# Arithmetic of GpSimd moved to VectorE before the feed-forward and in its last superblock of a hybrid decoder layer

## The chip, the cores and the metric

The kernel runs on one core of a Trainium2 chip. The metric is device time in microseconds (us) of one execution. Engines: TensorE (PE; its weight loads are listed as PEld), VectorE (DVE), ScalarE (ACT), GpSimd (POOL), SyncE (SP, which here only issues DMAs).

## The reference, cut to what matters

One decoder layer for a prompt of 2048 positions and 8 samples of 4 positions, all float32, width 1024:

```python
h = rms_norm(x, norm_mix); z = h @ w_in                       # u | xin | B | C, 512 each
y_ssm = s5_ssm(u, ...)                                        # 32 groups, 64 complex states, scan over time
y_ssm = gelu(y_ssm); y_ssm = y_ssm * sigmoid(y_ssm @ w_glu + b_glu)
y_conv = B * causal_dwconv(C * xin, conv_w)                   # width 3
x = x + concat(rms_norm(y_ssm), rms_norm(y_conv)) @ w_out
x = x + cross_attention(rms_norm(x, norm_xattn), k, v)        # 4 heads, 256 memory tokens
h = rms_norm(x, norm_ffn)
x = x + (gelu(causal_dwconv(h @ w_up)) * (h @ w_gate)) @ w_down   # 2816 wide
y = rms_norm(x, norm_final)
```

## The kernel before, in words

Positions are split into 5 pieces of up to 416 columns (`NPC`, `NP`). Every product is made at float32 accuracy from three matmuls (`mm3`, lines 365 to 367): each operand is split into a rounded `hi` and a remainder `lo`, and hi*hi, hi*lo and lo*hi are summed. So each weight tile and each activation tile costs a cast and a subtraction ahead of its matmuls:

- `Weights` (class of line 70 on): `issue` starts DMAs into 3 buffers `wraw` through SP, `split` has ACT cast a 128x1024 tile to `whi` (L94) and two subtractions make `wlo` in halves of 512 columns (L98). Both halves go to POOL, except where `share` is true: then the second goes to DVE. `pump` is called once per `block()`, `get` forces a split.
- `Acts`: `issue` loads a 128x416 tile `araw` through SP (L176), `pump` and `put` make `xh` on ACT and `xl`. Even tiles with a gain: `xh` by L161, `xl` by one DVE instruction (L162). Odd tiles: ACT first scales `araw` in place (L191), casts it (L158), and POOL subtracts (L159).

There is no scheduler: each engine runs its instructions in the order in which the code emits them, and waits at the first whose inputs are not ready. Side work is written as generators (`bg`, `slow`, `slow2`), and hooks between the matmuls advance them by a step. So the place of every side instruction among the matmuls is fixed when the program is built. All loads and most stores go through SP's queue, in that order too: a store whose data is late holds up the loads behind it.

Stages, by the time of the profile:

1. 0 to about 200 us, input projection of `u`. `p1_stream` transposes x on PE, splits it, and sums squares. `tables` computes the transition tables of the state space: per quarter `c` a complex product `pk` on DVE (`cmul`, L552 to L558), transposes on PE, and products `ogt`, `og` on POOL (`gtt`, L577). `rstd` makes row scales through diagonal tiles `dgh` on DVE and `dgl` on POOL (L426). `u_out` scales u on POOL (L786, L792) and stores it.
2. About 200 to 575 us, the other three projections, with a convolution per channel tile (`conv_in`, `conv_mid`, `conv_out`; the last multiplication of y is on POOL, L1272, and then y is stored). Beside it run `state_inputs` (`turn`, every third on POOL, L945 to L948; `scan_blocks` on DVE, L955), `toeplitz` (a copy `to` on POOL, L1039) and `state_outputs` (`back`, three DVE instructions and one on POOL, L1063 to L1067; `enter`, two additions `scat` on DVE and two on POOL, L1079, which PE waits for).
3. 575 to 675 us, keys and values of the memory (`memory`), the GLU (`p3_pre`) and its first piece; to about 900 us output projection (`residual_linear`), with `p3_pre` of the next piece beside it, partly on POOL.
4. To about 1500 us attention, then its output projection beside the samples' attention (`sample_attention`, `split` with a part on POOL, L1764).
5. From about 1500 us the feed-forward, 22 tiles of 128 channels for each of three superblocks of pieces (two pieces, two pieces, one). `f_down` multiplies into two PSUM banks `d` in turn; DVE adds each into `xac` (L2037), and PE cannot refill a bank before that. The third superblock, with one piece, uses each weight tile half as long as the others.

Of the kernel before, what the change touches and what calls it, by code (L numbers as in the profile page):

```python
# [71 lines left out]
class Weights:  # L72


    def __init__(self, nc, pool):
        self.nc, self.pool = nc, pool
        self.specs, self.raw, self.slots = [], {}, {}
        self.nraw = self.nsplit = self.nrel = self.now = 0
        self.age, self.share = 2, True
# [10 lines left out]
    def split(self):  # L90
# [31 lines left out]
class Acts:  # L122
# [5 lines left out]
    def __init__(self, nc, pool):  # L128
# [5 lines left out]
        self.age = 2  # L134
# [45 lines left out]
    def pump(self, n=1, force=False):  # L180
        self.now += 1
        self.issue()
        for _ in range(n):
# [5 lines left out]
            eng = self.nc.gpsimd if i % 2 else None  # L189
# [19 lines left out]
def tile_hymba_step(ctx: ExitStack, tc: tile.TileContext, I: dict, O: list):  # L209
# [201 lines left out]
    def rstd(pl, rs, acc, p, n, lag=3):  # L411
# [148 lines left out]
    def tables():  # L560
# [15 lines left out]
        def gtt(out, a, b, op):  # L576
            G.tensor_tensor(out=out, in0=a, in1=b, op=op)  # L577
# [106 lines left out]
        for m in (1, 2, 4):  # L684
# [3 lines left out]
                 pa[:, 0, m:m + 1, :].to_broadcast(sh), pa[:, 1, m:m + 1, :].to_broadcast(sh), sh, f"cm{m}", G)  # L688
            yield PAUSE
        G.tensor_copy(out=a4, in_=pa[:, :, 4, :])  # L690
        G.tensor_copy(out=mg, in_=mag)
        G.tensor_scalar(out=qc[:, 0], in0=cm, scalar1=1.0, scalar2=None, op0=ALU.add)
        G.tensor_copy(out=qc[:, 1], in_=sn)
# [85 lines left out]
    def u_out(p, us):  # L779
        yield PAUSE  # L780
        w, c0 = CW[p], CPP * p
        for j in range(4):
            u = us[j]
            cols = slice(j * 128, (j + 1) * 128)
            if p < 4:
                G.tensor_tensor(out=u, in0=u, in1=rs_p[p], op=ALU.mult)  # L786
                store(out=u_d[cols, :, c0:c0 + w], in_=u[:, 0:8 * w].rearrange("p (s c) -> p s c", s=8))
            else:
                e = ends[j % 2]
                for o, a, n in ((e[:, :, 0:w], 0, 8), (e[:, 0:NT, w:w + 8], 384, NT), (e[:, NT:8, w + 8:w + 16], 384, NT)):  # L790
                    z = slice(a, a + n * (w if a == 0 else 8))
                    G.tensor_tensor(out=o, in0=u[:, z].rearrange("p (s c) -> p s c", s=n),  # L792
# [18 lines left out]
    W.age, W.share = 6, False  # L811
# [145 lines left out]
    def state_inputs():  # L957
# [16 lines left out]
        def recur(upto, n):  # L974
# [5 lines left out]
            for _ in range(n):  # L980
# [3 lines left out]
                if turned < upto:  # L984
                    turn(turned, G if turned % 3 == 1 else V)
# [1162 lines left out]
```

## Time and profile before

| what | before |
|---|---|
| median of 3 runs | 3034.99 us (3028.71 to 3035.61) |
| the profiled execution | 3038.51 us, its span 3036.7 us |
| PE busy | 2891.9 us, 95% |
| DVE, POOL, ACT busy | 1474.0, 1152.2, 1112.6 us |
| PE busy, 0 to 683 us and after | about 86%, 98% |
| mean granted clock of PE | 0.977 |

The time is read from two things: where PE, the busiest engine, stands idle or at the lower of its two clock levels, and what ends those waits. "Released by" below means the semaphore event that came last before an instruction started.

### The profile page before, as it was taken

To read this page: it belongs to the slowest core of one execution; us is meant where nothing else is said; L and a number is where in the kernel's file an instruction comes from. 1 tells how busy PE (TensorE), PEld (TensorE's weight loads), DVE (VectorE), ACT (ScalarE), POOL (GpSimd) and SP (SyncE) were. 2 spreads that over 40 slices of the span, in tenths; PEclk is the share of its full clock that TensorE was granted. 3 is DMA by queue.
4 is the path that set the end of the run, shared out by engine and by line. 5 is a ranking of instruction groups with operands and counts; after the bars stand their busy time and mean duration, and the time that the engine had idled before them with its cause. 6 is when DMAs were issued, how large, how long until landed. Compare 5 with 4: busy or idle time off the path is not lost.

```text
span 3036.7 us, 41679 instructions
## 1 busy us (share of the span) xinstructions
PE 2891.9 (95%) x15536; PEld 2792.3 (92%) x15536; DVE 1474.0 (49%) x2704; ACT 1112.6 (37%) x2168; POOL 1152.2 (38%) x1264
## 2 busy tenths in 40 slices
PE   7877979989999999999999999999999999999998
PEld 7777969879999999989999999998999999999998
DVE  5758786354354343454543333435433433354544
ACT  5344333454544444342522222234222222243332
POOL 3664475353341004252523232233232233245653
PEclk9888989999999999999999999999999999999999
DMA  7564455364352123565632122124312122134331
GB/s 218 141 173 120 122 162 151 97 206 120 96 179 69 53 67 121 201 207 182 193 93 63 56 60 59 50 63 143 97 56 63 49 63 63 54 122 127 111 109 55
DMA packets 384073, 336.63 MB, mean 111 GB/s; under 512 B 77857, under 2 KB 357975, under 8 KB 383839
## 3 DMA queue, kind: packets, MB, share of 16 engines
q1 hardware_dynamic: 360303, 299.23, 33.4%
q10 hardware_dynamic: 23568, 34.75, 3.2%
q8 instruction: 122, 2.00, 0.3%
q14 instruction: 80, 0.66, 0.1%
HBM read 260.44 MB, written 75.56 MB: 111 GB/s over the span
## 4 chain that ended last, share of the span: by engine, by line
PE 56%; DVE 3%; DMA 2%; POOL 1%; ACT 1%; issue 1%; SPq 0%; ACTq 0%; POOLq 0%; DVEq 0%
PE g L366 5%; PE g L367 5%; PE g L365 5%; PE d L365 5%; PE u L366 5%; PE d L367 5%; PE d L366 5%; PE u L365 5%; PE u L367 5%; PE mm L366 3%; PE mm L365 3%; PE mm L367 3%; DVE t L1184 1%; DMA out_dram<-orow 1%; PE aux L366 0%
## 5 line engine op out<-in xcount | busy, mean ns | idle before, releaser
L98 POOL TENSOR_TENSOR wlo<-wraw,whi 128x512 fp32r<-128x512 f32 x489 | 644.9, 1342 | 900.3 <-ACT whi L94 840.4
L365 PE MATMUL mm<-xh,whi 128*128 128x416 f32 x1600 | 596.4, 373 | 9.0 <-ACT whi L94 3.9
L366 PE MATMUL mm<-xl,whi 128*128 128x416 f32 x1600 | 576.3, 360 | 6.8 <-POOL xl L159 6.8
L367 PE MATMUL mm<-xh,wlo 128*128 128x416 f32 x1600 | 572.3, 358 | 2.3 <-POOL wlo L98 2.3
L2037 DVE TENSOR_TENSOR xac<-d,xac 128x416 f32<-128x416 f32 x440 | 258.2, 590 | 252.5 <-PE d L367 248.5
L365 PEld LDWEIGHTS mm<-xh,whi 128*128 128x128 f32 x1600 | 311.5, 195 | 20.3 <-ACT whi L94 4.6
L365 PE MATMUL d<-acth,whi 128*128 128x416 f32 x880 | 311.7, 354 | 17.0 <-DVE xac L2037 15.8
L366 PEld LDWEIGHTS mm<-xl,whi 128*128 128x128 f32 x1600 | 311.2, 194 | 12.9 <-POOL xl L159 8.3
L367 PEld LDWEIGHTS mm<-xh,wlo 128*128 128x128 f32 x1600 | 310.8, 194 | 6.6 <-POOL wlo L98 3.7
L366 PE MATMUL u<-xl,whi 128*128 128x416 f32 x880 | 311.9, 354 | 1.6 <-POOL xl L159 0.9
L366 PE MATMUL g<-xl,whi 128*128 128x416 f32 x880 | 312.2, 355 | 0.0
L365 PE MATMUL g<-xh,whi 128*128 128x416 f32 x880 | 311.0, 353 | 0.0
L365 PE MATMUL u<-xh,whi 128*128 128x416 f32 x880 | 309.8, 352 | 0.2
L367 PE MATMUL g<-xh,wlo 128*128 128x416 f32 x880 | 309.8, 352 | 0.0
L367 PE MATMUL d<-acth,wlo 128*128 128x416 f32 x880 | 309.7, 352 | 0.0
L367 PE MATMUL u<-xh,wlo 128*128 128x416 f32 x880 | 308.6, 351 | 0.0
L366 PE MATMUL d<-actl,whi 128*128 128x416 f32 x880 | 308.0, 350 | 0.2 <-DVE actl L2018 0.2
L94 ACT CAST whi<-wraw 128x1024 fp32r<-128x1024 f32 x256 | 266.5, 1046 | 81.6 <-PE d L366 40.7
L1184 DVE SCALAR_TENSOR_TENSOR t<-E,par,t 128x416 f32<-128x416 f32 (+1 forms) x220 | 154.6, 702 | 267.2 <-ACT t L2005 264.6
L159 POOL TENSOR_TENSOR xl<-araw,xh 128x416 fp32r<-128x416 f32 x100 | 114.6, 1149 | 369.0 <-ACT xh L158 339.4
L2010 ACT ACTIVATE t<-t 128x416 f32<-128x416 f32 x110 | 60.7, 552 | 413.0 <-DVE t L1184 342.3
L2014 DVE TENSOR_TENSOR t<-t,g 128x416 f32<-128x416 f32 x110 | 64.4, 586 | 261.0 <-PE g L367 260.9
(461 smaller groups left out, 5025.1 us busy)
## 6 DMA issues: line engine op xcount, KB each, us to landing
wraw<-in_w_up_dram SPq DMA_DIRECT2D x66, 512.0 KB
wraw<-in_w_gate_dram SPq DMA_DIRECT2D x66, 512.0 KB
wraw<-in_w_down_dram SPq DMA_DIRECT2D x66, 512.0 KB
araw<-x SPq DMA_DIRECT2D x120, 208.0 KB
xres<-x SPq DMA_DIRECT2D x80, 208.0 KB
x<-xo ACTq DMA_DIRECT2D x80, 208.0 KB
uc<-u_d SPq DMA_DIRECT2D x64, 136.0 KB
x<-xT ACTq DMA_DIRECT2D x40, 208.0 KB
```

Of the source, the lines that this page charges most:

```text
L94: self.nc.scalar.copy(out=hi, in_=r)
L98: eng.tensor_tensor(out=lo[:, s], in0=r[:, s], in1=hi[:, s], op=ALU.subtract)
L159: (eng or nc.vector).tensor_tensor(out=lo[:, 0:n], in0=src, in1=hi[:, 0:n], op=ALU.subtract)
L365: PE.matmul(ps, lhsT=wh, rhs=xh, start=start, stop=False)
L366: PE.matmul(ps, lhsT=wh, rhs=xl, start=False, stop=False)
L367: PE.matmul(ps, lhsT=wl, rhs=xh, start=False, stop=stop)
L1184: V.scalar_tensor_tensor(out=out[:, 0:n], in0=E[:, tap * w:tap * w + n], scalar=c, in1=out[:, 0:n], op0=ALU.mult, op1=ALU.add)
L2010: S.activation(out=t, in_=t, func=AF.Gelu_apprx_tanh)
L2014: V.tensor_tensor(out=t, in0=t, in1=ps_[:, 0:NP], op=ALU.mult)
L2037: V.tensor_tensor(out=x, in0=ps[:, 0:NP], in1=x, op=ALU.add)
```

## The change

DVE now does what POOL did before the feed-forward: all `wlo` and `xl`, the tables, `dgl`, the scaling of u and y, all `turn`, `back` and `enter`, the sums and products of `p3_pre`, the parts of the samples' `split`. Two kinds of copies go to ACT: `to` and `s0s`. With `A.odd` empty, odd tiles are treated as even ones, so ACT no longer scales `araw` in place (60 instructions of L191). POOL keeps small copies at the ends of convolutions (L1198 to L1202), the small z tiles of the samples, and one copy of the GLU's weights. At the feed-forward `W.eng` and `A.odd` become POOL, which there does what it did before; at the third superblock `W.eng` becomes DVE.

```diff
@@ Weights, Acts @@
-        self.age, self.share = 2, True
+        self.age, self.eng = 2, nc.vector
...
-            eng = self.nc.vector if c and self.share else self.nc.gpsimd
-            eng.tensor_tensor(out=lo[:, s], in0=r[:, s], in1=hi[:, s], op=ALU.subtract)
+            self.eng.tensor_tensor(out=lo[:, s], in0=r[:, s], in1=hi[:, s], op=ALU.subtract)
...
-            eng = self.nc.gpsimd if i % 2 else None
+            eng = self.odd if i % 2 else None
@@ rstd @@
-            for eng, dg, src in ((V, dgs[0], ch), (G, dgs[1], cl)):
-                eng.tensor_tensor(out=dg[0:r, o:o + k * r].rearrange("p (g c) -> p g c", g=k),
+            for dg, src in ((dgs[0], ch), (dgs[1], cl)):
+                V.tensor_tensor(out=dg[0:r, o:o + k * r].rearrange("p (g c) -> p g c", g=k),
@@ tables @@
         def gtt(out, a, b, op):
-            G.tensor_tensor(out=out, in0=a, in1=b, op=op)
+            V.tensor_tensor(out=out, in0=a, in1=b, op=op)
...
@@ u_out @@
-                G.tensor_tensor(out=u, in0=u, in1=rs_p[p], op=ALU.mult)
+                V.tensor_tensor(out=u, in0=u, in1=rs_p[p], op=ALU.mult)
...
@@ state_inputs @@
-                    turn(turned, G if turned % 3 == 1 else V)
+                    turn(turned)
...
-                G.tensor_copy(out=sv[i * 64:(i + 1) * 64, a], in_=s0[a * 64:(a + 1) * 64, i])
+                S.copy(out=sv[i * 64:(i + 1) * 64, a], in_=s0[a * 64:(a + 1) * 64, i])
@@ toeplitz @@
-            G.tensor_copy(out=to, in_=trs.pop(c).rearrange("p t (g q) -> p g t q", q=16)[:, :, ::-1])
+            S.copy(out=to, in_=trs.pop(c).rearrange("p t (g q) -> p g t q", q=16)[:, :, ::-1])
@@ back, enter, conv_out @@
-            G.tensor_tensor(out=x, in0=x, in1=ph[:, 0, c].unsqueeze(1).unsqueeze(1).to_broadcast(SQ), op=ALU.mult)
+            V.tensor_tensor(out=x, in0=x, in1=ph[:, 0, c].unsqueeze(1).unsqueeze(1).to_broadcast(SQ), op=ALU.mult)
...
-                    (G if r else V).tensor_tensor(out=sc[r * 64:(r + 1) * 64, a, 1:256], in0=m1[h, r, 0:255],
+                    V.tensor_tensor(out=sc[r * 64:(r + 1) * 64, a, 1:256], in0=m1[h, r, 0:255],
...
-            G.tensor_tensor(out=y, in0=y, in1=rs_p[p], op=ALU.mult)
+            V.tensor_tensor(out=y, in0=y, in1=rs_p[p], op=ALU.mult)
@@ p3_pre and its call, sample_attention @@
-            A.put(ys[j], eng=G if j % 2 else V)
+            A.put(ys[j], eng=V)
...
-            nxt = bg.add(p3_pre(ORDER3[i + 1], G))
+            nxt = bg.add(p3_pre(ORDER3[i + 1]))
...
-                (G if i else V).tensor_tensor(out=lo[:, i:i + n], in0=src, in1=hi[:, i:i + n], op=ALU.subtract)
+                V.tensor_tensor(out=lo[:, i:i + n], in0=src, in1=hi[:, i:i + n], op=ALU.subtract)
@@ feed-forward @@
+    W.eng = A.odd = G
...
             if f == 0:
+                if len(ps_sb) == 1:
+                    W.eng = V
```

Where this lands in the order of DVE is shown at three places (line numbers of the changed code are lower by one or two).

Stage 1, DVE between two quarters of `tables`; before, `pk` of the next quarter follows the splits and sums of x directly:

```order
L395 TENSOR_TENSOR acc<-acc,sq 128x416
L162 SCALAR_TENSOR_TENSOR xl<-mm,par,xh 128x416
L395 TENSOR_TENSOR acc<-acc,sq 128x416
L552 TENSOR_TENSOR cpk<-parev,bb 128x512
L553 TENSOR_TENSOR pk<-parev,bb 128x512
```

and in the change:

```order
L161 SCALAR_TENSOR_TENSOR xl<-mm,par,xh 128x416
L394 TENSOR_TENSOR acc<-acc,sq 128x416
L576 TENSOR_TENSOR ogt<-ct,pat 128x512
L576 TENSOR_TENSOR ogt<-ctn,pat 128x512
L576 TENSOR_TENSOR og<-ogt 64x4x128 x2
L576 TENSOR_TENSOR ogt<-ctn,pat 128x512 x2
L576 TENSOR_TENSOR og<-ogt 64x4x128 x2
L161 SCALAR_TENSOR_TENSOR xl<-mm,par,xh 128x416
L394 TENSOR_TENSOR acc<-acc,sq 128x416
L551 TENSOR_TENSOR cpk<-parev,bb 128x512
```

Eight instructions of POOL stand now in DVE's queue between one quarter and the next, around a split of x that PE needs.

Stage 2, DVE in `state_outputs`, one group pair (`enter`, then `back` of the next); before:

```order
L162 SCALAR_TENSOR_TENSOR xl<-araw,par,xh 128x416
L1074 MEMSET scat 128x2
L1079 TENSOR_TENSOR scat<-st,mb 64x255 x2
L1063 TENSOR_TENSOR mc<-ek,rp 128x512
L1065 TENSOR_TENSOR st<-st,mc 128x2x256
L1066 TENSOR_TENSOR mb<-st,ph 128x512
```

and in the change:

```order
L161 SCALAR_TENSOR_TENSOR xl<-araw,par,xh 128x416
L1073 MEMSET scat 128x2
L1078 TENSOR_TENSOR scat<-st,mb 64x255 x4
L1062 TENSOR_TENSOR mc<-ek,rp 128x512
L1064 TENSOR_TENSOR st<-st,mc 128x2x256
L1065 TENSOR_TENSOR mb<-st,ph 128x512
L1066 TENSOR_TENSOR st<-st,ph 128x2x256
L97 TENSOR_TENSOR wlo<-wraw,whi 128x512 x2
```

The chain that went from DVE to POOL (last product of `back`) and on to both engines (`enter`) is on DVE alone, and weight splits stand between.

Third superblock, DVE in one `f_down`; before:

```order
L2037 TENSOR_TENSOR xac<-d,xac 128x416 x4
L1184 SCALAR_TENSOR_TENSOR t<-E,par,t 128x384
L1188 SCALAR_TENSOR_TENSOR t<-E,par,t 128x32
L2037 TENSOR_TENSOR xac<-d,xac 128x416 x2
L1184 SCALAR_TENSOR_TENSOR t<-E,par,t 128x384
L1188 SCALAR_TENSOR_TENSOR t<-E,par,t 128x32
L2037 TENSOR_TENSOR xac<-d,xac 128x416 x2
```

and in the change:

```order
L2035 TENSOR_TENSOR xac<-d,xac 128x416 x2
L97 TENSOR_TENSOR wlo<-wraw,whi 128x512 x2
L2035 TENSOR_TENSOR xac<-d,xac 128x416 x2
L1183 SCALAR_TENSOR_TENSOR t<-E,par,t 128x384
L1187 SCALAR_TENSOR_TENSOR t<-E,par,t 128x32
L97 TENSOR_TENSOR wlo<-wraw,whi 128x512 x2
L2035 TENSOR_TENSOR xac<-d,xac 128x416 x2
L1183 SCALAR_TENSOR_TENSOR t<-E,par,t 128x384
L1187 SCALAR_TENSOR_TENSOR t<-E,par,t 128x32
L2035 TENSOR_TENSOR xac<-d,xac 128x416 x2
```

Two weight splits of two instructions each now stand between the additions that empty the PSUM banks.

## Rows read from the trace of the kernel before

**Rows 1.** The page's first part: busy time and share of each engine.
```profile
PE 2891.9 (95%) x15536; PEld 2792.3 (92%) x15536; DVE 1474.0 (49%) x2704; ACT 1112.6 (37%) x2168; POOL 1152.2 (38%) x1264
```

**Rows 2.** Stretches: length, busy time (instructions) PE, PEld, DVE, ACT, POOL, PE's clock, DMA.
```profile
75.00:200.00 125.00, 103.20 (x557) 95.15 (x557) 77.62 (x138) 43.71 (x93) 79.69 (x89) 0.87 0.56 151
200.00:350.00 150.00, 127.10 (x593) 119.41 (x593) 126.96 (x266) 61.87 (x137) 67.39 (x66) 0.90 0.48 132
350.00:500.00 150.00, 127.23 (x593) 117.59 (x592) 119.83 (x176) 52.37 (x117) 97.13 (x94) 0.90 0.52 156
2670.00:3000.00 330.00, 315.33 (x1680) 305.10 (x1679) 169.35 (x280) 124.11 (x217) 176.41 (x191) 1.00 0.38 113
```

**Rows 3.** Waits of PE, 0 to 500 us: total us, times, longest.
```profile
PE aux L994 <- DMA gc<-g_d: 13.9, 4, 4.8
PE aux L1108 <- DMA tcn<-to_d: 12.4, 5, 5.0
PE aux L1109 <- POOL scat L1079: 4.1, 1, 4.1
```

**Rows 4.** Waits of SP's queue, 200 to 500 us.
```profile
SPq L256 <- POOL y L1272: 76.7, 14, 12.3
```

**Rows 5.** POOL by line, 200 to 500 us: count | busy us, mean ns | idle before.
```profile
L159 POOL TENSOR_TENSOR xl<-araw,xh 128x416 fp32r<-128x416 f32 x30 | 36.8, 1232 | 31.5 <-ACT xh L158 29.5 <-DMA araw<-x 2.0
L98 POOL TENSOR_TENSOR wlo<-wraw,whi 128x512 fp32r<-128x512 f32 x20 | 28.6, 1456 | 3.9 <-DMA wraw<-in_w_in_dram 3.9
L1079 POOL TENSOR_TENSOR scat<-st,mb 64x255 f32<-64x255 f32 x30 | 26.1, 869 | 2.3
L1067 POOL TENSOR_TENSOR st<-st,ph 128x512 f32<-128x512 f32 x15 | 20.4, 1358 | 24.6 <-DVE mb L1066 20.3 <-DVE scat L1074 4.2
L1272 POOL TENSOR_TENSOR y<-y,rs 128x416 f32<-128x416 f32 x14 | 19.5, 1392 | 31.6 <-DVE y L1271 31.6
```

**Rows 6.** DVE by line, 200 to 500 us.
```profile
L955 DVE TENSOR_TENSOR_SCAN st<-dz,st 128x256 f32<-128x256 f32 x32 | 33.4, 1083 | 10.5 <-ACT dz L952 6.7 <-POOL st L948 3.8
L1079 DVE TENSOR_TENSOR scat<-st,mb 64x255 f32<-64x255 f32 x30 | 31.3, 1043 | 14.6 <-POOL st L1067 14.1
L162 DVE SCALAR_TENSOR_TENSOR xl<-araw,par,xh 128x416 fp32r<-128x416 f32 x29 | 23.9, 833 | 16.9 <-ACT xh L161 16.7
```

**Rows 7.** DVE, single lines: shortest/median/longest ns of an instruction, first and last start.
```profile
L1079 DVE TENSOR_TENSOR scat<-st,mb x32: 416/1181/1484, 374.8 to 504.4; 64x255 f32<-64x255 f32 x32
L955 DVE TENSOR_TENSOR_SCAN st<-dz,st x32: 657/1028/1700, 236.8 to 326.6; 128x256 f32<-128x256 f32 x32
L162 DVE SCALAR_TENSOR_TENSOR xl<-araw,par,xh x60: 620/651/1658, 179.6 to 1127.1; 128x416 fp32r<-128x416 f32 x60
L162 DVE SCALAR_TENSOR_TENSOR xl<-mm,par,xh x40: 571/651/652, 8.6 to 171.8; 128x416 fp32r<-128x416 f32 x40
L98 DVE TENSOR_TENSOR wlo<-wraw,whi x23: 671/692/2671, 12.1 to 676.8; 128x512 fp32r<-128x512 f32 x23
```

**Rows 8.** DVE's timeline at 103 us: start us, us.
```profile
103.31 0.64 DVE L162 SCALAR_TENSOR_TENSOR xl<-mm,par,xh 128x416 fp32r<-128x416 f32 x1
103.87 0.57 DVE L395 TENSOR_TENSOR acc<-acc,sq 128x416 f32<-128x416 f32 x1
```

**Rows 9.** DVE by line, 75 to 200 us.
```profile
L395 DVE TENSOR_TENSOR acc<-acc,sq 128x416 f32<-128x416 f32 x19 | 15.2, 800 | 0.0
L554 DVE TENSOR_TENSOR pk<-pk,cpk 128x512 f32<-128x512 f32 x4 | 4.4, 1112 | 0.1
```

**Rows 10.** Waits of PE, 500 to 2670 us.
```profile
PE mm L366 <- POOL xl L159: 3.0, 4, 0.7
PE aux L366 <- POOL skl L1764: 2.8, 3, 1.9
```

**Rows 11.** DVE's timeline in one `f_down` of the third superblock.
```profile
2817.88 1.43 DVE L1184 SCALAR_TENSOR_TENSOR t<-E,par,t 128x384 f32<-128x384 f32 x1
2821.40 0.60 DVE L1184 SCALAR_TENSOR_TENSOR t<-E,par,t 128x384 f32<-128x384 f32 x1
```

More of the change, by code (lines that the diff above doesn't have):

```diff
@@ L133, in __init__ @@
         self.late = self.tick = None
-        self.age = 2
+        self.age, self.odd = 2, None
     def order(self, i):
@@ L687, in tables @@
                  pa[:, 0, 1:m + 1, :], pa[:, 1, 1:m + 1, :],
-                 pa[:, 0, m:m + 1, :].to_broadcast(sh), pa[:, 1, m:m + 1, :].to_broadcast(sh), sh, f"cm{m}", G)
+                 pa[:, 0, m:m + 1, :].to_broadcast(sh), pa[:, 1, m:m + 1, :].to_broadcast(sh), sh, f"cm{m}")
             yield PAUSE
[L690 to L693, printed above, removed]
+        V.tensor_copy(out=a4, in_=pa[:, :, 4, :])
+        V.tensor_copy(out=mg, in_=mag)
+        V.tensor_scalar(out=qc[:, 0], in0=cm, scalar1=1.0, scalar2=None, op0=ALU.add)
+        V.tensor_copy(out=qc[:, 1], in_=sn)
         par_ = pre.tile([128, 2, 16, 8], F32, name="parev")
-        G.tensor_copy(out=par_, in_=pa[:, :, 0:8, :].rearrange("p r k g -> p r g k")[:, :, :, ::-1])
+        V.tensor_copy(out=par_, in_=pa[:, :, 0:8, :].rearrange("p r k g -> p r g k")[:, :, :, ::-1])
         pat = pre.tile([128, 2, 16, 8], F32, name="pat")
-        G.tensor_copy(out=pat, in_=pa[:, :, 1:9, :].rearrange("p r k g -> p r g k"))
+        V.tensor_copy(out=pat, in_=pa[:, :, 1:9, :].rearrange("p r k g -> p r g k"))
         for _ in range(3):
@@ L791, in u_out @@
                     z = slice(a, a + n * (w if a == 0 else 8))
-                    G.tensor_tensor(out=o, in0=u[:, z].rearrange("p (s c) -> p s c", s=n),
+                    V.tensor_tensor(out=o, in0=u[:, z].rearrange("p (s c) -> p s c", s=n),
                                     in1=rs_p[p][:, z].rearrange("p (s c) -> p s c", s=n), op=ALU.mult)
@@ L810, in tile_hymba_step @@
     run(xs1)
-    W.age, W.share = 6, False
+    W.age = 6
     for p in range(NPC):
@@ L940, in blocks, with turn @@
         return st[:, :, c, 0:256].rearrange("p r (k j) -> p r k j", j=16)
-    def turn(c, eng):
+    def turn(c):
         x, m2 = blocks(c), product_tile("b")
-        eng.tensor_tensor(out=m2, in0=x[:, ::-1], in1=ph[:, 1, c].unsqueeze(1).unsqueeze(1).to_broadcast(SQ), op=ALU.mult)
-        eng.tensor_tensor(out=x, in0=x, in1=ph[:, 0, c].unsqueeze(1).unsqueeze(1).to_broadcast(SQ), op=ALU.mult)
+        V.tensor_tensor(out=m2, in0=x[:, ::-1], in1=ph[:, 1, c].unsqueeze(1).unsqueeze(1).to_broadcast(SQ), op=ALU.mult)
+        V.tensor_tensor(out=x, in0=x, in1=ph[:, 0, c].unsqueeze(1).unsqueeze(1).to_broadcast(SQ), op=ALU.mult)
         for r, op in ((0, ALU.add), (1, ALU.subtract)):
-            eng.tensor_tensor(out=x[:, r], in0=x[:, r], in1=m2[:, r], op=op)
+            V.tensor_tensor(out=x[:, r], in0=x[:, r], in1=m2[:, r], op=op)
     def scan_blocks(c):
@@ L1066, in back @@
             V.tensor_tensor(out=m2, in0=x[:, ::-1], in1=ph[:, 1, c].unsqueeze(1).unsqueeze(1).to_broadcast(SQ), op=ALU.mult)
-            G.tensor_tensor(out=x, in0=x, in1=ph[:, 0, c].unsqueeze(1).unsqueeze(1).to_broadcast(SQ), op=ALU.mult)
+            V.tensor_tensor(out=x, in0=x, in1=ph[:, 0, c].unsqueeze(1).unsqueeze(1).to_broadcast(SQ), op=ALU.mult)
             parts[c] = [m.rearrange("p r k j -> p r (k j)") for m in (x, m2)]
@@ L1387, in p3_pre @@
                 yield STALL
-            A.put(yc[j], eng=G if j % 2 else V)
+            A.put(yc[j], eng=V)
             yield
@@ L1464, in residual_linear @@
                     A.done.add((("x1", p), j))
-            W.share = False
         if nxt is not None:
@@ L1567, in tile_hymba_step @@
     pre = bg.add(p3_pre(ORDER3[0]))
-    W.share = True
     memory("k", k_d, False, mem)
@@ L1599, in values @@
                 S.copy(out=vh[:, t, cs], in_=r)
-                G.tensor_tensor(out=vl[:, t, cs], in0=r, in1=vh[:, t, cs], op=ALU.subtract)
+                V.tensor_tensor(out=vl[:, t, cs], in0=r, in1=vh[:, t, cs], op=ALU.subtract)
     p4b = []
```

## The prediction

> **What bounds the kernel now.** I read the page's totals first, then the stretches by stage, then who ends PE's waits where it stands idle, then the lines of DVE and POOL in those stretches, and last single lines for their shortest and longest instruction. The totals say that PE is busy 95% of the span while DVE has 49% [rows 1], so nothing that only lightens DVE or POOL on average pays. The stretches say where it can: from 200 to 500 us PE is busy 127.1 and 127.2 of 150 us, idle 45.7 in all, at a granted clock of 0.90, a mix of its two levels, 1.2 and 2.4 GHz; and there DVE is busy 127.0 and 119.8 of 150 [rows 2]. So in that stretch DVE, in order, is nearly full, and PE waits for what comes through it. PE's own waits there are put down mostly to loads, gc with 13.9 us and tcn with 12.4, and one of 4.1 to POOL's scat [rows 3]. The loads are late because SP's queue stood 76.7 us behind stores of y, which waited for POOL [rows 4]. The feed-forward is no place for a gain in its first two superblocks, which the change leaves alone; in the third PE is idle 14.7 of 330 us [rows 2].
>
> The second thing to see is what POOL does to DVE. A split of x by L162 takes 571 to 652 ns, all 40 of them, where its input comes from PSUM; the same instruction with both inputs in SBUF goes up to 1658 ns [rows 7]. The `scat` addition takes 416 at the least and 1181 in the median; a scan 657 and 1028 [rows 7]. So DVE instructions that read two SBUF operands are stretched by up to about 1 us, as long as one instruction of POOL [rows 5], and DVE's 247 us are not 247 us of its own work.
>
> **The change, part by part.**
>
> *Second stage, 200 to 500 us.* Five groups of POOL hold 131.4 of its 164.5 us there: xl 36.8, wlo 28.6, scat 26.1, the last product of `back` 20.4, y 19.5 [rows 2, 5]. On DVE I price them at undisturbed durations: 30 x 0.651 = 19.5, 20 x 0.692 = 13.8, 30 x 0.416 = 12.5, 15 x 0.692 = 10.4 (512 elements, as wlo), 14 x 0.651 = 9.1 [rows 5, 7], together 65.3, half of POOL's time. Of the other 33.1 us two thirds move (the rest is copies that stay or go to ACT), 11 us at that ratio. Added: 76.3. DVE sheds what POOL stretched: scans 32 x (1083 - 657) = 13.6, scat 30 x (1043 - 416) = 18.8, xl 29 x (833 - 651) = 5.3, together 37.7 [rows 6, 7]. That makes 246.8 - 37.7 + 76.3 = 285 us at most. Two things lower it. DVE's other 158 us hold stretched instructions too; the three groups lose 43%, and I allow the others 10%, 16 us. And neighbours overlap: an xl of 0.64 us is followed after 0.56 [rows 8], 0.08 for each of the 109 instructions, 9 us. The low end is 260; I take 262, since both effects stand in rows. To this comes idle time. DVE had 53 us of it; 17.9 ended by POOL [rows 6] go, and of the remaining 35 I keep 15, because a fuller queue meets more inputs that are already there. So 277 us in place of 300: **-23**. Bounds: 260 with hardly a gap, -39; 285 with 30 us of gaps, +15.
>
> The Trainium skill, page "Perfetto Trace Analysis", section Optimizing Scalar/DVE Operations, speaks against this part: if DVE is saturated, handing work to ScalarE or even GpSimd may make sense, though it adds that the two share an SBUF read port, so that it might not help. By its first half, taking work back onto an engine busy 127 of 150 us would lengthen the stage, to the time of the second rival below; by the rows on shedding it would not, and I side with the rows.
>
> On ACT the scaling of odd tiles goes, the copies `to` and `s0s` come; ACT is busy 62 and 52 of 150 us [rows 2], and DVE covers either, so I cost it at nothing. If that cover went, ACT's lighter queue would be a gain. On SP the loads keep their place, but y is ready 14 x (1.39 - 0.65) = 10 us sooner in sum; this is inside the 23.
>
> *First stage, 75 to 200 us.* DVE has 77.6, POOL 79.7 of 125 us [rows 2]. At the same ratio DVE gains 40; it sheds 19 x 0.23 = 4.4 in the sums acc (0.57 undisturbed) and 4 x (1.11 - 0.69) = 1.7 in one of the six lines of `pk` [rows 8, 9]. That is 111 of 125 at most; with the other lines and 0.08 for each of POOL's 89 instructions about 100. Where `ogt` and `og` now stand ahead of `pk` and of the splits, PE can be made to wait for the tables; in exchange POOL's tail disappears. I take **+2**, bounds -8 and +12.
>
> *500 to 2670 us.* PE's waits for POOL's xl (3.0) and skl (2.8) [rows 10] turn into shorter ones; half is given back where DVE, busier, is late with the additions that empty PSUM between halves of the output projection: **-3**, bounds -6 and +6. The first two superblocks: nothing changes.
>
> *Third superblock.* Eleven down-products share 14.7 us of idle PE. In one, a tap of the convolution took 1.43 us on DVE with POOL at work, 0.60 without [rows 11], and held up the next addition. That goes, but two weight splits of 2 x 0.692 us each now stand between additions. The queue has gaps to swallow about half: **0** net. Bounds: -10, most of the idle time gone, and +15, 11 x (2.8 - 0.8 - 0.6).
>
> *Sum.* -23 + 2 - 3 + 0 = -24. The profiled execution took 3038.5 us (span 3036.7 and 1.8 around it), so 3014.5; it lies 3.5 us over the median of the three runs, so **3011 us** as a median. About 0.3%, 9 us, is what a measurement of this kernel can tell from no change. Own range of this case: 2993 to 3028.
>
> **The rivals.**
>
> 1. *The loads bind.* SP's wait for y is set by PE's last matmul of the channel tile, since POOL itself waited 31.6 us for DVE's y before it [rows 5]; the 26.3 us of gc and tcn [rows 3] then stay, and DVE's freed time fills with waiting. Left are scat's 4.1 and some of rows 10: about -5, **3030 us**. For it: these loads are the largest waits of PE. Against it: behind that y stood POOL's queue, which is gone.
> 2. *DVE saturates.* One queue holds splits that PE needs behind bulk arithmetic. If the idle time stays near the old level because each wait of DVE now delays everything, 285 + 30 = 315 in the second stage (+15) and 111 + 25 = 136 in the first (+11), less 3: +23, **3058 us**. It decides from the point at which busy and idle of DVE exceed 300 and 125 us, that is idle over 15 us at the upper sum, over 38 at mine. For it: DVE is already at 85% from 200 to 350 us. Against it: the shed time is measured on the very lines that remain.
> 3. *DVE becomes free enough that PE runs.* The lower sum, 260, with hardly a gap (-39), the first stage -8, rows 10 in full (-6), the third superblock -5: -58, **2977 us**. For it: one late load causes the next wait, so waits vanish together, and PE's clock of 0.87 to 0.90 rises with fewer pauses. Against it: DVE cannot run without gaps while it waits for ACT's casts [rows 6].
>
> That the change would not do what it says can be left aside: the order of the built program shows POOL without these instructions and DVE with them.
>
> **How the numbers follow.** Forecast 0.55, the loads bind 0.17, saturation 0.14, PE runs 0.14. The prediction is the likeliest, 3011. The range 2975 to 3042 holds the forecast, the third rival at 2977 and the first, and leaves out saturation and the ends. Faster by over 0.3%: forecast 0.53 and the third rival 0.14, 0.67. Within: 0.17 and 0.02 of the forecast, 0.19. Slower: 0.14.
>
> **What would show it right or wrong.** Right: longest `scat`, scan and xl on DVE near their shortest before; DVE's busy time from 200 to 500 us between 260 and 285 in a shorter stage; SP without long waits for y; the first stage within 10 us of its old length; one down-product of the third superblock still with about 1 us of wait. Wrong: DVE instructions still stretched with POOL idle, which would mean that something else stretched them; PE's waits for gc and tcn unchanged (first rival); new waits of PE for `pk`, xi or xo behind wlo (second).

## The result, and the profile after

The changed kernel takes **2993.98 us** in the median of 4 runs (2991.74 to 2995.75); the kernel before, on the same chip, takes 3032.52 (3028.71 to 3035.61). The ratio is 0.9871, with a 95% interval of 0.9856 to 0.9886: faster by 38.5 us, where 24 were forecast. The profiled execution took 2993.58 us, its span is 2991.8.

The page's first part, for the changed kernel; it answers to [rows 1]:

```profile
PE 2870.4 (96%) x15536; PEld 2773.0 (93%) x15536; DVE 1610.5 (54%) x3307; ACT 1087.1 (36%) x2120; POOL 455.0 (15%) x649
```

DVE has 136 us more, POOL 697 less, PE 21 less for the same number of matmuls. Where the time went is read from five stages, cut at the same matmul in both traces: the first product of the second stage, its last one, the end of the attention part, the first and the last superblocks of the feed-forward. The columns are those of [rows 2]: length, then busy time of PE, PEld, DVE, ACT, POOL, then PE's granted clock, the DMA engines' share and GB/s. Before:

```profile
0.00:187.10 187.10, 153.42 (x813) 139.57 (x813) 115.85 (x249) 81.80 (x164) 98.27 (x105) 0.90 0.65 178
187.10:579.10 392.00, 342.46 (x1642) 323.01 (x1642) 277.06 (x495) 140.72 (x306) 199.09 (x203) 0.92 0.46 133
579.10:1460.70 881.60, 854.82 (x4934) 823.62 (x4933) 410.26 (x814) 397.59 (x829) 291.90 (x386) 0.99 0.44 139
1461.30:2692.80 1231.50, 1221.23 (x6432) 1196.87 (x6432) 501.65 (x862) 362.93 (x640) 383.16 (x374) 1.00 0.25 74
2692.80:3036.70 343.90, 319.38 (x1719) 308.60 (x1717) 168.61 (x284) 129.52 (x230) 179.73 (x196) 0.99 0.36 108
```

And after:

```profile
0.00:178.80 178.80, 145.58 (x812) 132.54 (x812) 133.55 (x343) 81.07 (x163) 2.20 (x11) 0.94 0.68 186
178.80:548.50 369.70, 333.66 (x1641) 315.66 (x1642) 289.00 (x660) 126.73 (x279) 4.70 (x27) 0.95 0.49 142
548.50:1415.80 867.30, 849.18 (x4936) 819.17 (x4935) 480.13 (x1037) 386.94 (x809) 44.24 (x164) 0.99 0.45 142
1416.30:2643.30 1227.00, 1217.74 (x6431) 1195.66 (x6431) 500.99 (x864) 362.74 (x640) 380.88 (x372) 1.00 0.25 74
2643.30:2991.80 348.50, 323.71 (x1719) 309.51 (x1718) 206.30 (x404) 129.64 (x230) 23.03 (x75) 0.98 0.35 107
```

So the lengths change by -8.3, -22.3, -14.3, -4.5 and +4.6 us, -44.8 together. This is more than the medians' 38.5 because the profiled execution of before lies 6.0 us above its median and that of after 0.4 below. In the second stage DVE is busy 11.9 us longer, and POOL has 194 us less; the 22.3 us are 13.5 of PE's idle time (49.5 to 36.0) and 8.8 of its busy time, where the granted clock rose from 0.92 to 0.95 between the levels 1.2 and 2.4 GHz.

Single lines of DVE after the change, shortest/median/longest; they answer to [rows 7]:

```profile
L1078 DVE TENSOR_TENSOR scat<-st,mb x64: 408/419/422, 354.4 to 475.5; 64x255 f32<-64x255 f32 x64
L954 DVE TENSOR_TENSOR_SCAN st<-dz,st x32: 661/674/692, 226.1 to 309.1; 128x256 f32<-128x256 f32 x32
L161 DVE SCALAR_TENSOR_TENSOR xl<-araw,par,xh x120: 622/646/654, 174.0 to 1098.8; 128x416 fp32r<-128x416 f32 x120
```

On these lines nothing of the stretching is left: the longest scat is 422 ns, where the median was 1181; the longest scan 692, where it was 1700.

PE's largest waits in the second stage after, and SP's longest from 190 to 475 us, for [rows 3, 4]:

```profile
PE aux L993 <- DMA gc<-g_d: 15.5, 5, 7.2
PE aux L1107 <- DMA tcn<-to_d: 9.1, 4, 5.7
PE aux L513 <- ACT st L996: 4.4, 1, 4.4
PE aux L1107 <- ACT yg L1109: 3.6, 1, 3.6
...
SPq L255 <- DVE y L1271: 82.6, 14, 11.6
```

Before, two more stood beside those of [rows 3]:

```profile
PE aux L994 <- ACT dz L952: 6.4, 1, 6.4
PE mm L366 <- POOL xl L159: 3.9, 1, 3.9
```

The waits for gc and tcn are nearly what they were, 24.6 us where they were 26.3, and SP stands longer behind y than before. What went are the waits for POOL's scat and xl and for ACT's dz; the waits for ACT's st and yg grew, from 2.5 to 9.3 us.

### The profile page after: what moved, and what is told of

The parts are those of the page before. It is cut to its first block, busy times and chain, and to the rows that moved or that the text cites. A ratio compares the mean times of both kernels' runs of the same rounds, so it can differ in the third digit from the quotient of the medians.

```text
span 2991.8 us, 41377 instructions
## 1 busy us (share of the span) xinstructions
PE 2870.4 (96%) x15536; PEld 2773.0 (93%) x15536; DVE 1610.5 (54%) x3307; ACT 1087.1 (36%) x2120; POOL 455.0 (15%) x649
## 4 chain that ended last, share of the span: by engine, by line
PE 70%; DVE 4%; DMA 3%; ACT 2%; issue 1%; POOL 1%; SPq 0%; ACTq 0%; POOLq 0%; DVEq 0%
PE mm L365 7%; PE mm L364 7%; PE mm L366 7%; PE g L365 5%; PE g L364 5%; PE g L366 5%; PE u L365 5%; PE u L366 5%; PE u L364 5%; PE d L364 5%; PE d L366 5%; PE d L365 5%; DVE wlo L97 1%; DMA out_dram<-orow 1%; DMA x<-xo 1%
## 5 line engine op out<-in xcount | busy, mean ns | idle before, releaser
L364 PE MATMUL mm<-xh,whi 128*128 128x416 f32 x1600 | 588.9, 368 | 9.3 <-ACT whi L94 5.6
L365 PE MATMUL mm<-xl,whi 128*128 128x416 f32 x1600 | 569.3, 356 | 0.6 <-DVE xl L161 0.6
L366 PE MATMUL mm<-xh,wlo 128*128 128x416 f32 x1600 | 566.0, 354 | 0.1
L97 POOL TENSOR_TENSOR wlo<-wraw,whi 128x512 fp32r<-128x512 f32 x268 | 345.0, 1309 | 617.7 <-ACT whi L94 586.3
L364 PEld LDWEIGHTS mm<-xh,whi 128*128 128x128 f32 x1600 | 306.8, 192 | 18.8 <-ACT whi L94 6.6
L1183 DVE SCALAR_TENSOR_TENSOR t<-E,par,t 128x416 f32<-128x416 f32 (+1 forms) x220 | 147.7, 671 | 251.5 <-ACT t L2003 248.6
L97 DVE TENSOR_TENSOR wlo<-wraw,whi 128x512 fp32r<-128x512 f32 x244 | 156.7, 685 | 66.6 <-ACT whi L94 66.5
L364 PEld LDWEIGHTS d<-acth,whi 128*128 128x128 f32 x880 | 165.7, 188 | 27.8 <-DVE xac L2035 25.1
```

The source lines that it names most:

```text
L97: self.eng.tensor_tensor(out=lo[:, s], in0=r[:, s], in1=hi[:, s], op=ALU.subtract)
L364: PE.matmul(ps, lhsT=wh, rhs=xh, start=start, stop=False)
L365: PE.matmul(ps, lhsT=wh, rhs=xl, start=False, stop=False)
L366: PE.matmul(ps, lhsT=wl, rhs=xh, start=False, stop=stop)
L1183: V.scalar_tensor_tensor(out=out[:, 0:n], in0=E[:, tap * w:tap * w + n], scalar=c, in1=out[:, 0:n], op0=ALU.mult, op1=ALU.add)
```

## The experiments

Twelve kernels, told as ratios to the kernel before on the same chip where that matters. One thing has to be known for reading them: in the eight profiled executions whose first stage is the program of the changed kernel, or differs from it only by memsets and one-column copies on POOL or by states in the second stage, that stage took 173.9 to 181.7 us. The second stage took 369.7 to 373.0 us in the three whose program there is that of the changed kernel. A few us in a median can come from there, so each verdict rests on the stage that its edit touches, and there on one profiled execution.

### Whose reads stretch DVE: work on POOL that nobody waits for

`pool_reads`, against the changed kernel, called after every split up to the memory stage, twice for a weight tile (165 times; of this edit and the next only the body of the added function is shown):

```diff
+        G.tensor_tensor(out=idle[:, 0:n], in0=hi[:, 0:n], in1=lo[:, 0:n], op=ALU.subtract)
```

> The changed kernel with POOL given work that nobody waits for: after each split of a weight or activation tile, up to the memory stage, a subtraction of two SBUF operands of 128x416 into a tile that is never read. All of the useful arithmetic stays where the change put it, and the output is the same. Theory (C): what the change gained there is above all the end of the stretching of DVE by POOL's reads; so scan and scat additions on DVE, 674 and 419 ns in the changed kernel, go up again (mean of the scan over 800 ns), DVE is busy 20 us or more longer from 200 to 500 us, and the time rises by 8 to 20 us, to 3002 to 3014. Rival (D): the gain comes from shorter instructions and from hand-offs between DVE and POOL that are gone; DVE's instructions keep their lengths, and the time stays within 3 us of 2994.

`pool_writes`, in the same places:

```diff
+        G.tensor_copy(out=idle[:, 0:1], in_=lo[:, 0:1])
+        for _ in range(3):
+            G.memset(idle, 0.0)
```

> The same places, but POOL's extra work only writes: a copy of one column, which waits for the same split, and then three memsets of 128x416, for about as long as the subtraction. The output is the same. Theory (C), stretching by reads of two operands in SBUF: DVE's scan and scat stay near 674 and 419 ns and the time within 3 us of 2994. Rival (E), any busy POOL slows DVE or the semaphores: as with the subtractions, 3002 to 3014.

`dve_reads` is `pool_reads` with `V` in the place of `G`.

> The subtractions into a tile that is never read, as in pool_reads, but executed by DVE, so that POOL stays idle. In pool_reads the 165 instructions on POOL cost 62 us and made DVE busy 100 us longer, 0.61 us for each. Theory (F): a POOL instruction with two SBUF operands takes as much of DVE as if DVE executed it itself; then this kernel is busy 165 x 0.57 = 94 us longer on DVE and ends within 12 us of pool_reads, 3044 to 3068. Rival (G): most of the 62 us came from DVE being stopped at bad moments or from tiles held longer, and the plain work costs less than half: below 3025.

Measured: 3056.10 us with POOL's subtractions, 2992.69 with its memsets, 3044.17 with DVE's subtractions. The second stage of the three, in this order:

```profile
194.70:619.30 424.60, 348.55 (x1642) 323.27 (x1642) 362.69 (x659) 125.77 (x279) 138.04 (x131) 0.91 0.42 123
```

```profile
176.90:552.80 375.90, 335.49 (x1642) 316.74 (x1643) 290.28 (x660) 127.00 (x279) 174.07 (x442) 0.95 0.48 140
```

```profile
194.50:607.80 413.30, 348.77 (x1641) 324.17 (x1641) 349.20 (x764) 126.08 (x279) 4.72 (x27) 0.91 0.44 127
```

DVE's busy time is 289.0 us in the changed kernel. POOL's subtractions, with not one instruction added on DVE, make it 362.7; memsets that keep POOL busier (174 us against 138) leave it at 290.3, though the stage is 3 to 6 us longer than in the executions without them; the same subtractions on DVE itself make it 349.2. The lines that are stretched are those of [rows 7], here with `pool_reads` and below it `pool_writes`:

```profile
L966 DVE TENSOR_TENSOR_SCAN st<-dz,st x32: 661/690/1600, 249.7 to 347.8; 128x256 f32<-128x256 f32 x32
L1090 DVE TENSOR_TENSOR scat<-st,mb x64: 409/421/1294, 397.5 to 547.3; 64x255 f32<-64x255 f32 x64
```

```profile
L967 DVE TENSOR_TENSOR_SCAN st<-dz,st x32: 661/672/692, 225.7 to 309.6; 128x256 f32<-128x256 f32 x32
L1091 DVE TENSOR_TENSOR scat<-st,mb x64: 408/419/442, 354.7 to 479.1; 64x255 f32<-64x255 f32 x64
```

With `pool_reads` the means are 1053 ns for the scan and 636 for scat, where the changed kernel has 674 and 418, though the medians hardly moved. So it is POOL's reading of operands that stretches DVE, and a POOL busy with writing does not; theory C holds against D and E, but I had its price too low by a factor of three at least, 8 to 20 us for 62. Over the whole program DVE is busy 1710.7 us against 1610.5, 0.61 us for each of the 165 instructions of POOL, which last about 1.27. On DVE the same instruction takes 0.588. So theory F holds, just inside its range: this subtraction, given to POOL, took as much of DVE as if DVE did it, and lasted twice as long. Why `pool_reads` is 12 us slower than `dve_reads` was not taken apart. The Trainium skill, page "SBUF — State Buffer", section Who interferes with whom, says that a DVE instruction with two SBUF inputs contends with a GpSimd instruction that reads SBUF, not with one that only writes it. The trace agrees on both: 1600 and 1294 ns with the reads, 692 and 442 with the writes.

### Each part of the change put back

> The changed kernel with the arithmetic of the state space and of y in the second stage back on POOL (every third turn, the last product of back, half of enter, the scaling of y); splits and tables stay on DVE. Theory (F), with the hand-offs as the gain: DVE's busy time from 200 to 500 us is about the same as in the changed kernel, since what DVE sheds it pays in stretching, but the waits of DVE and PE for POOL return (before, DVE waited 17.9 us and PE 4.1): 12 to 20 us slower, 3006 to 3014, nearly all in the second stage, the first as in the changed kernel. Rival (H): what gained were the splits; 2992 to 3000.

> The changed kernel with the splits of weights and activations up to the feed-forward as before (odd activation tiles and the weight halves on POOL, with ACT's extra scaling); the rest stays on DVE, and the third superblock as changed. Theory (F): these are 40 us of POOL in the first stage and 65 in the second; PE waits for some of them, and DVE is stretched by about what it sheds; 8 to 15 us slower, 3002 to 3009, spread over both stages. Rival (H): the splits carry most of the 38.5 us: 3015 to 3025.

> The changed kernel with only the first stage's tables, the diagonal tiles dgl and the scaling of u back on POOL. The first stage gained 8.2 us in the change, where the prediction had a loss of 2. Theory (F): the tables are work that PE waits for little; put back, they stretch DVE as much as they relieve it, so 2992 to 2998, within the first stage. Rival (I): the whole 8.2 us come from them, through POOL's tail before the second stage: 3001 to 3004.

```diff
@@ states_back @@
-                    turn(turned)
+                    turn(turned, G if turned % 3 == 1 else V)
...
-            V.tensor_tensor(out=y, in0=y, in1=rs_p[p], op=ALU.mult)
+            G.tensor_tensor(out=y, in0=y, in1=rs_p[p], op=ALU.mult)
@@ splits_back @@
-            self.eng.tensor_tensor(out=lo[:, s], in0=r[:, s], in1=hi[:, s], op=ALU.subtract)
+            eng = self.eng or (self.nc.vector if c and self.share else self.nc.gpsimd)
+            eng.tensor_tensor(out=lo[:, s], in0=r[:, s], in1=hi[:, s], op=ALU.subtract)
...
-        self.age, self.odd = 2, None
+        self.age, self.odd = 2, nc.gpsimd
...
@@ tables_back @@
         def gtt(out, a, b, op):
-            V.tensor_tensor(out=out, in0=a, in1=b, op=op)
+            G.tensor_tensor(out=out, in0=a, in1=b, op=op)
...
```

Measured medians: 2994.82 us, ratio 0.9876 (0.9860 to 0.9892); 3008.24, 0.9921 (0.9906 to 0.9936); 3001.80, 0.9895 (0.9879 to 0.9912). By stages of the profiled executions, as lengths:

| stage | before | after | states back | splits back | tables back |
|---|---|---|---|---|---|
| first | 187.1 | 178.8 | 178.6 | 177.8 | 186.8 |
| second | 392.0 | 369.7 | 381.1 | 375.9 | 373.2 |
| memory to attention's end | 881.6 | 867.3 | 864.6 | 878.7 | 870.9 |

By these single executions the three parts add up: put back one at a time they return 6.8 of the first stage's 8.3 us, 21.1 of the second's 22.3 and 12.3 of the third's 14.3. The tables are the first stage (rival I), the states half of the second, the splits most of the third, where I had expected the splits in the first two. In the medians the parts return less, 0.8, 14.3 and 7.8 us of the 38.5.

The states are the one part whose median (2994.8, in the range of rival H) does not show what its profile shows. So they were tried from the other side, as the only thing changed in the kernel before:

> The kernel before with one part of the change alone: the arithmetic of the state space and of y in the second stage on DVE, all else as before. Putting this part back into the changed kernel cost 0.8 us in the medians, though 11 us in the second stage of its profiled execution, with 2.6 gained later. Theory (L): DVE pays for these instructions about what POOL's reads cost it, and the hand-offs saved are worth a few us: 3028 to 3034 against 3033 before. Rival (M): the part is worth its 11 us in the second stage, hidden by chance in the first comparison: 3018 to 3026.

3024.12 us against 3032.29, ratio 0.9969 (0.9957 to 0.9981), by 12 runs: rival M. The second stage, with the states on POOL (`states_back`) and with them alone on DVE (`states_alone`):

```profile
178.60:559.70 381.10, 335.15 (x1642) 316.68 (x1642) 288.88 (x573) 127.00 (x279) 106.33 (x114) 0.94 0.47 138
```

```profile
187.20:568.10 380.90, 336.10 (x1642) 316.79 (x1641) 292.90 (x582) 140.04 (x306) 100.42 (x116) 0.94 0.47 138
```

Each differs from its neighbour by 11 us. With the states back on POOL DVE is busy 288.9 us, with them on DVE 289.0: half of theory F was exact, what DVE sheds it pays. So the states' 11 us are not DVE's work there. DVE's idle time ended by POOL, 19.4 us in the stage before and none after, is 9.5 us with the states back, so the hand-offs are the likelier cause, though no kernel took them apart from the work. Why the median of `states_back` shows so little is open; its runs spread from 2989.9 to 3000.0, and the profiled one is the longest, so its 11 us may be too many; `states_alone` has 8.2 us in the medians.

### The first stage

It gained where a loss of 2 was forecast. From the matmul that starts at 90 us before to the stage's end, before, after, and with the tables back:

```profile
90.00:187.10 97.10, 80.53 (x442) 74.16 (x440) 63.00 (x105) 32.35 (x70) 59.74 (x48) 0.86 0.52 148
```

```profile
89.50:178.80 89.30, 75.29 (x441) 68.73 (x438) 76.02 (x155) 31.53 (x69) 0.00 (x0) 0.94 0.60 160
```

```profile
86.30:186.80 100.50, 83.52 (x442) 76.93 (x439) 64.28 (x105) 31.85 (x69) 59.36 (x48) 0.83 0.49 144
```

POOL's 59.7 us became 13.0 more on DVE, less than a quarter. Here too DVE's instructions had been stretched; these are the copies of `ct` into `cpad`, before and after:

```profile
L743 DVE COPY cpad<-ct x8: 175/805/1284, 104.4 to 166.2; 64x64 f32<-64x64 f32 x8
L742 DVE COPY cpad<-ct x8: 175/186/194, 101.0 to 160.2; 64x64 f32<-64x64 f32 x8
```

With the tables back their median is 804 again. They read one operand, so the stretching is not confined to instructions that read two. PE waited for pk 7.3 us before and 7.4 after, so what I had feared did not come; the waits for `cpad`, behind these copies, fell from 5.3 to 1.9. Of the 7.8 us between the first two rows 2.6 are idle time and 5.2 are PE's busy time for the same matmuls at a clock of 0.94 for 0.86. One piece of before shows the slow level: PE, after a wait of 2.8 us for cpad, is busy all but half a microsecond of these ten, and yet does 37 matmuls, at 0.53, near the level of 1.2 GHz. In a piece after the change, behind a wait of 2.0 us for pk, it does 58 (not the same ones), at 0.83. That shorter waits raised the clock is read from such pieces; no kernel tested it apart.

```profile
125.00:135.00 10.00, 9.52 (x37) 9.21 (x38) 2.94 (x7) 1.46 (x3) 9.78 (x10) 0.53 0.39 103
```

```profile
135.00:145.00 10.00, 10.00 (x58) 9.38 (x59) 7.69 (x18) 1.90 (x5) 0.00 (x0) 0.83 0.18 53
```

### The third superblock

Here the change lost 4.6 us. DVE's timeline in its first down-product, then PE's and ACT's rows of the same place:

```profile
2675.65 1.13 DVE L2035 TENSOR_TENSOR xac<-d,xac 128x416 f32<-128x416 f32 x2
2676.70 1.28 DVE L97 TENSOR_TENSOR wlo<-wraw,whi 128x512 fp32r<-128x512 f32 x2
2677.90 0.58 DVE L1927 TENSOR_TENSOR acc<-acc,sq 128x416 f32<-128x416 f32 x1
2678.40 1.08 DVE L2035 TENSOR_TENSOR xac<-d,xac 128x416 f32<-128x416 f32 x2
...
2683.49 1.29 DVE L97 TENSOR_TENSOR wlo<-wraw,whi 128x512 fp32r<-128x512 f32 x2 [3.31 <-ACT whi L94]
2684.70 0.58 DVE L1927 TENSOR_TENSOR acc<-acc,sq 128x416 f32<-128x416 f32 x1
2685.20 1.08 DVE L2035 TENSOR_TENSOR xac<-d,xac 128x416 f32<-128x416 f32 x2
...
2685.84 0.72 PE L364 MATMUL d<-acth,whi 128*128 128x416 f32 x1 [4.25 <-DVE xac L2035]
...
2682.41 1.04 ACT L94 CAST whi<-wraw 128x1024 fp32r<-128x1024 f32 x1 [5.83 <-DMA wraw<-in_w_down_dram]
```

A weight load is late, ACT stands 5.83 us at its cast, DVE 3.31 us at the subtraction behind the cast, and the addition that empties PE's bank is queued behind that: PE waits 4.25 us. The load was as late before, where ACT waited 5.32 us and POOL 3.52:

```profile
2729.86 1.05 ACT L94 CAST whi<-wraw 128x1024 fp32r<-128x1024 f32 x1 [5.32 <-DMA wraw<-in_w_down_dram]
...
2730.98 2.90 POOL L98 TENSOR_TENSOR wlo<-wraw,whi 128x512 fp32r<-128x512 f32 x2 [3.52 <-ACT whi L94]
```

POOL's queue held nothing that PE needed soon; PE's longest wait for xac was 1.5 us. In total PE waited for xac even longer before, 11.8 us where it is 9.6 after; the loss lies around the one long wait. From the superblock's first product to the one that starts 44.2 us later in before, the columns as above, before and after:

```profile
2692.80:2737.00 44.20, 42.34 (x241) 39.92 (x240) 27.97 (x52) 23.64 (x43) 20.03 (x23) 1.00 0.52 161
```

```profile
2643.30:2696.30 53.00, 45.38 (x242) 42.52 (x242) 33.90 (x66) 23.78 (x43) 2.85 (x9) 0.94 0.44 135
```

PE is idle 5.8 us longer there, and busy 3.0 us longer for the same matmuls, at a granted clock of 0.94 for 1.00. The rest of the superblock is 4.2 us shorter than before. Two kernels test this:

```diff
@@ third_on_pool @@
-                if len(ps_sb) == 1:
-                    W.eng = V
@@ third_later @@
+            if f == 4 and len(ps_sb) == 1:
+                W.eng = V
             if f == 0:
-                if len(ps_sb) == 1:
-                    W.eng = V
```

> The changed kernel with the weight splits of the third superblock left on POOL, as before. Theory (A): the change lost time there, because DVE, in order, stands at a weight split whose cast on ACT waits for a late load, while the additions that empty the PSUM banks queue behind it; between the landmarks of the traces the third superblock is 4.6 us longer than before, so this kernel gives about 2989.5 us, and PE's longest wait for xac there falls from 4.2 us to about 1.5. Rival (B): the extra 4.6 us come from what lies around (the placement of loads, the clock), and POOL's splits stretch DVE's taps again: no gain, 2992 to 2997.

> The changed kernel, with the switch of the weight splits to DVE only from the fifth tile of the third superblock on, after the normalisation of the superblock before has been written. Theory (A): the loss of about 8.5 us lies wholly in the first tiles, where a late weight load stops DVE, and from there on DVE's splits gain about 3.5 us; so about 2985.5 us, faster than both the changed kernel (by 8) and the one with all of these splits on POOL (by 4). Rival (B): the late load recurs with any split on DVE: 2990 to 2996.

2988.12 us, ratio 0.9852 (0.9829 to 0.9875), and 2979.61 us, 0.9818 (0.9801 to 0.9836). The third superblock is 343.3 us long in the first and 339.6 in the second, where before had 343.9 and the change 348.5. The total wait for xac in `third_later`, with 9.6 us and a longest of 4.2 in the changed kernel:

```profile
PE d L364 <- DVE xac L2035: 4.6, 9, 1.2
```

Theory A holds by the stage: the loss lies in the first tiles, and from the fifth on DVE's splits gain 3.7 us. The median of `third_on_pool` alone is not clear of the changed kernel's. `third_later` is the fastest kernel of the study, 14.4 us under the changed kernel, but only 8.9 of them are the third superblock; 4.9 are its first stage of 173.9 us, which the edit does not touch.

### Three attempts at the waits that stayed

Each is an edit of `third_later`.

```diff
@@ y_store_later @@
-            store(out=yc_d[p][:, ct_, :], in_=y)
+            held.append((yc_d[p][:, ct_, :], y))
...
+            if k == 5 and held:
+                store(*held.pop())
@@ two_dz @@
-    dz = sp_.tile([128, 16, 16], F32, name="dz")
+    dz, dz1 = (sp_.tile([128, 16, 16], F32, name=f"dz{i}") for i in range(2))
...
+        d = dz1 if c % 2 else dz
@@ copies_on_pool @@
-            S.copy(out=to, in_=trs.pop(c).rearrange("p t (g q) -> p g t q", q=16)[:, :, ::-1])
+            G.tensor_copy(out=to, in_=trs.pop(c).rearrange("p t (g q) -> p g t q", q=16)[:, :, ::-1])
```

> The version third_later (2979.6 us), with the store of each y of the second stage issued five hooks into the next channel tile, in place of right after y's last multiplication. In the changed kernel SP still waited 82.6 us for y in that stage (before 76.7), and PE still waited 24.7 us for gc and tcn (before 26.3). Theory (J), the first rival of the prediction as far as it goes: y is late because PE's last matmul and DVE's queue are ahead of it, whoever multiplies, and the loads behind the store are late with it; so here SP's wait for y falls below 20 us, PE's for gc and tcn below 12, and the time by 8 to 15 us, to 2965 to 2972. Rival (K): gc and tcn are late because their tiles come free late or u and the tables are stored late; no change, 2976 to 2983.

2985.92 us, ratio 0.9839 (0.9823 to 0.9855): no gain, theory J fell. SP's wait for y is down to 0.7 us; it stands at the next thing that is not ready, a buffer for x, 101.4 us where `third_later` has 52.1:

```profile
SPq L175 <- DVE xl L161: 101.4, 45, 14.2
```

gc and tcn still cost PE 22.6 us, for 25.4, and the second stage is 368.8 us long, within a microsecond of the changed kernel's 369.7.

> The version third_later (2979.6 us), with two tiles dz in turn for the scans of the second stage, where there was one. In the changed kernel and in third_later ACT stands at the copy into dz until DVE has done the scan before, up to 5 us, and the copies of st behind it on ACT are late for PE, which waits 5.8 to 6.4 us for them. Theory (N): PE's waits for st fall below 2 us, those for gc by as much as their tiles come free sooner, and the time by 4 to 10 us, to 2970 to 2976. Rival (O): DVE, busy 289 of 370 us in the stage, sets the pace, and the wait turns up at gc: 2977 to 2983.

2986.57 us, 0.9843 (0.9829 to 0.9856). PE's waits for st are 6.6 us where they were 6.2, and the stage is 370.4 us long, inside the spread: theory N fell, rival O is left.

> third_later, with the two kinds of copies that the change gave to ACT back on POOL. Theory (C): a copy on POOL reads one operand, and there are only 12 of them, so DVE hardly notices; ACT is 5 us less busy in the second stage. 2975 to 2983, no difference that can be measured; the copies to on POOL take near 0.6 us, as their shortest before, with DVE's 128x512 instructions at their shortest too. Rival: the place on ACT cost PE its waits for st and yg (about 10 us): 2968 to 2974.

2988.06 us, 0.9846 (0.9832 to 0.9859). The second stage, which holds the edit, has 372.6 us for 373.0, and DVE is busy 290.8 for 288.9: no difference there. These three lie 6 to 8 us over `third_later` in the median, above the ranges of all their theories and rivals, and their first stages, which none of them touches, took 180.4 to 181.7 us for 173.9. What makes the first stage differ so is open.

## Why the prediction was right or wrong

**Second stage, -23 forecast for 200 to 500 us; -18.8 measured for the same matmuls, -22.3 for the whole stage.** The cause was right: DVE's 247 us were not its own work, as `pool_reads` and `pool_writes` show, and the lines that were priced shed what was forecast, 13.6 for the scans, 18.8 for scat, 5.3 for xl. By mean times in the whole stage before and after it was 33.4 - 20.3 = 13.1, 32 x (1.017 - 0.418) = 19.2, 38 x (0.826 - 0.644) = 6.9. But two terms of the sum were mis-sized, in opposite directions. This stretch of the changed kernel holds the matmuls of 200 to 500 us before [rows 2]:

```profile
188.30:469.50 281.20, 245.51 (x1184) 229.65 (x1183) 244.00 (x564) 104.95 (x236) 3.23 (x18) 0.94 0.54 156
```

DVE's busy time, forecast to rise by 15 us, fell from 246.8 to 244.0, with some 120 instructions more. If these cost the 76.3 us of the forecast, 79 went, where the working had 63 (37.7 shed by three lines, 16 by all others, 9 of overlap). A line that stood only among the others shed 8.6 us, 16 x (1.231 - 0.692):

```profile
L1063 DVE TENSOR_TENSOR mc<-ek,rp 128x512 f32<-128x512 f32 x16 | 19.7, 1231 | 0.5
L1062 DVE TENSOR_TENSOR mc<-ek,rp 128x512 f32<-128x512 f32 x16 | 11.1, 692 | 0.5
```

DVE's idle time was to fall from 53 to 15 us and fell to 37.2. The 17.9 us ended by POOL went; of the other 35 nothing went on balance, so the step that failed is "a fuller queue meets more inputs that are already there". Beside the forecast's busy time of 262 such idle time would have left no gain to speak of, by the second rival's own mark of 38. So it is partly luck that the sum came near: one error made up for the other. And 8.8 of the 18.8 us are PE's busy time at a granted clock of 0.94 for 0.90, which only the third rival had named.

**What I said of SP's queue in it fell.** I called the loads late because SP stood behind y, which waited for POOL. SP stood there as long with y on DVE, and with y's store moved away it stood elsewhere. So the first rival was right that gc and tcn would stay, and wrong that DVE's gain would be lost to them: POOL's scat and xl (8.0 us) and ACT's dz (6.4, behind the chain of scans) left PE's list.

**First stage, +2 forecast, -8.3 measured.** DVE's load was right, about 100 of 125 us forecast for 75 to 200 us and 98.1 of 120.8 for the same matmuls; the step that failed is what it does to PE, "PE can be made to wait for the tables". Copies that PE waits for were no longer stretched, and PE's clock rose, which the sum had no term for; 7.8 of the 8.3 us are PE's busy time. `tables_back` returns 8.0 us.

**500 to 2670 us, -3 forecast, about -19 measured** (-14.3 to the attention's end, -4.5 in the first two superblocks). The failed step is the bound of 6: I priced only PE's waits for xl and skl [rows 10] and had half of them given back. Waits for wlo (3.4 us) and acc (1.4) on POOL went too, and PE nowhere stood at the additions that I feared; only its wait for ACT's whi rose, from 2.6 to 5.4 us. Of the 14.3 us 5.6 are PE's busy time, with the clock at 0.99 in both rows, so what shortened it is open. The splits are most of the 14.3 (`splits_back`, +11.4). The -4.5 us, in superblocks whose instructions are the same, were tested by nothing; other versions took 1220.6 to 1229.4 us there.

**Third superblock, 0 forecast, +4.6 measured**, inside its bounds. From the fifth tile on DVE's queue takes the splits without a loss; what failed is that I counted the splits' durations between additions and not what the splits themselves wait for.

**The sum.** 2994 lies 17 us under the forecast and inside the range; the direction and the cause were right. The main term came near by two errors that largely cancelled, the first stage had the wrong sign, and the term to 2670 us was too small by 16. Of the signs that it named, scat, scan and xl at their shortest came; DVE's 260 to 285 us in a shorter stage did not (244.0), nor did SP without long waits for y. The second rival, saturation, did not come at 289 us of DVE, but `dve_reads` shows it to be near: 96 us more on DVE, and 50 us are lost. The Trainium skill, page "Perfetto Trace Analysis", section Optimizing Scalar/DVE Operations, had the case for leaving work on GpSimd, with the warning that, because of the shared read port, it might not help. The runs decide for the warning: 0.61 us of DVE for each instruction that POOL took.

## What to carry to other kernels

Before counting an engine's free time as free, look at the shortest, the mean and the longest of its neighbour's instructions of one form: where they lie far apart, moving work between the two may move nothing. The median can miss it, as with `pool_reads` (scan 661, 690 and 1600 ns, mean 1053), and so can the shortest, where every instruction is stretched: `mc` took 1100 ns at the least before and 693 in the median after. Before putting work into a queue that PE waits on, ask what that work itself waits for: a load that came as late left PE waiting for xac 1.5 us at most with its split on POOL, and 4.25 with it on DVE. And a wait of an in-order DMA queue names the first thing that is not ready, not the only one.

## What the runs showed of the hardware

- 165 subtractions on POOL that nobody waits for cost 62 us of the kernel's time and 100 us of DVE's, more than the same work on DVE (50 and 96 us). As many one-column copies with 495 memsets, 271 us of POOL, cost nothing that can be measured in the time, and 4.7 us of DVE's.
- DVE copies of 64x64 with one operand took 175 to 1284 ns beside POOL's arithmetic in the first stage, and 175 to 194 without it.
- In the first stage before, pieces of 10 us that begin with or hold pauses of PE of 1.6 to 3.7 us have a granted clock of 0.53 to 0.68. Over the first two stages more of the gain, 16.6 of 30.6 us, is PE's busy time for the same matmuls at a higher granted clock than is idle time.
